# A two-layer hybrid decoder step: output gate stored as its silu, ten stream steps, the last taps and a score product moved

## The chip, the core and the metric

The kernel runs on one core of a Trainium2 chip. The metric is the device time of one execution in microseconds (us), the median of several. A core has a matrix engine (TensorE, PE in the profile; PEld is its weight load), three engines for element-wise work (VectorE or DVE, ScalarE or ACT, GpSimd or POOL) and SyncE (SP), which only issues transfers (DMA) here; ACT issues some too. Each engine carries out its own row of instructions in order, and waits where one needs a result of another engine or of a transfer.

## What is computed

Two layers over 1,104 tokens: 1,040 of a prompt and 64 of eight running sequences. In each layer the normalised input is projected to 8,260 columns, which feed three branches. Cut to what the change touches:

```
u = rmsnorm(h, norm_g) @ w_in + b_in           # af, aq, v(ai), az, ga, gg, bz, q, k, v, indexer, cz, gate
# branch A, HGRN2, four heads of 128 channels
q, k = silu(aq), (1 - lb) * sigmoid(-af);  o = gated linear recurrence(q, k, v, log f)
out_a = (norm(o) * silu(az)) @ w_pa            # az: the output gate
# branch B, Conformer convolution
y = silu(layernorm(conv31(ga * sigmoid(gg)) + conv_b))
out_b = ((y @ conv_pw) * silu(bz)) @ w_pb      # "pointwise products"
# branch C, sparse attention
s = sum over 4 heads of relu(qi_h . ki) * wi_h # indexer: scores; the 256 best keys are kept
out_c = (attention over the kept keys * silu(cz)) @ w_pc
h = h + (gate_a*out_a + gate_b*out_b + gate_c*out_c) @ w_out
```

## The kernel before

Channels lie on the 128 partitions, tokens along the free dimension, in three groups of 384, 384 and 336 (`NTS`). fp32 products are made of three fp32r ones (high by high, low by high, high by low). That is the dense **stream** (`stream`, L346): for each chunk of 128 channels and each group 24 matmuls into one of two PSUM buffers (`mm`), eight steps of three (L396). ACT evicts the buffer with the bias into an SBUF buffer (`sp`, L206 from L401) and, behind the third group, issues the store of the chunk to HBM itself (L411: `afD`, `aqD`, `vD`, `azD`, `czD`, ...). The weights of a chunk are split by ACT (`wh`, L271) and POOL (`wl`, L272). For a `cz` chunk the stream also makes the silu: a second ACT pass over the PSUM buffer gives the sigmoid into another `sp` buffer, and POOL multiplies.

PE's row is written out in program order. All other stages run on PE between pieces of the stream: `fill(key)` issues as many stream steps as the table `FILL` has for that key. Long DVE work is metered in the same way: `SIDE` has a budget in ns for each place, in which `taps(key)` issues taps of the convolution and `masks(key)` steps of the mask building. The order on DVE is that of the program in most stages, and that on ACT in a few; a scheduler sets the rest, so a changed table moves rows on these engines too.

The stages of a layer, in order, as far as they matter:

- **Indexer** (`indexer`, L759). For six blocks of queries and four heads PE makes scores (`lg`), ACT the relu (`rl`), and DVE multiplies by the head's weight and adds up (`SC`; the first head by L840, the others by L842). Then four copies and four subtractions make `qt8` (L853 to L858). For the eight running sequences the cached keys are gathered, scored and summed over heads by a product of PE (`gather`, L860 to L871) in two halves: DVE adds `lg` and `ac` to `SC` (L870, L871) after each. L908 is PE's next product and reuses the PSUM buffer `lg`. All the while DVE runs the **taps** of the convolution: 31 for each of four channel chunks, L1594 over the prompt and L1595 over the sequences, into `cy`. The last tap of a chunk is followed by its store `yD[c]` on SP (L1597).
- **Layer norm of the convolution** (`conv_norm`, L1602). For each token group SP loads `ny` from `yD`, two channel chunks a time (L1608), POOL adds the four chunks (L1611, L1612: `nsq`), PE sums over partitions (L1615), DVE and ACT go on, and SP stores the result (L1634).
- **Four heads** of the recurrence (`hgrn_head`, L1349). SP loads `hG`, `hQ`, `hT_` and `az`; ACT makes three sigmoids; POOL `sg = Q * sigmoid(Q)` (L1371); ACT and POOL `az * sigmoid(az)` (`sz`, L1376 to L1378); DVE products (L1400 to L1402), which ACT casts (`hl`, L1407).
- **Pointwise products** (`conv_out`, L1662). Three groups by four chunks of 12 matmuls on `BH` and `BL` (L289); DVE multiplies each result by silu(bz) (`bzt`, L1693), SP stores it; mask steps stand between (L1031 to L1040).
- **Attention** (`attention`, L1044). q goes through the rotary embedding (`rope_q`, L727: loads, DVE, stores on SP), k and v come back from HBM (`kr` and `vr`, L1056 and L1057, on ACT's queue), PE transposes `kr` (L1063), and the first scores are L1107.

## Time and profile before

| | |
|---|---|
| Median of 3 executions | 2865.78 us (2864.01 to 2873.34) |
| The profiled execution | 2876.56 us; its span in the trace 2874.7 us |
| Mean granted TensorE clock | 0.985 of full |
| PE busy | 2741.0 us, 95% of the span |
| DVE, ACT, POOL busy | 70%, 47%, 44% |
| PE waiting for ACT to evict a stream buffer | 33.0 us in 20 places, the longest 5.5 |

All rows come from the profiled execution, and times in them count from the start of its span. A row of a timeline has the start, the length, the engine, the line, the operation, the tiles written and read, shapes, and in brackets the idle time of that engine just before and what ended it. A row with the engine SPq or ACTq is the issue of a transfer. The first layer ends at about half of the span; the second repeats its stages.

### The profile page before, as it was taken

How to read it: one execution, taken by the hardware profiler on the slowest of the kernel's cores; microseconds unless marked ns; L12 is line 12 of the kernel's file. 1: busy time of each engine (PE TensorE's matmuls, PEld its weight loads, DVE VectorE, ACT ScalarE, POOL GpSimd, SP SyncE). 2: the span in 40 equal slices, each digit the busy share in tenths (PEclk: the TensorE clock that was granted, in tenths of full speed). 3: DMA queues.
4: the chain of work that ended last, by engine and by line, in shares of the span. 5: the costliest groups of instructions: out<-in, count | busy, mean ns of one | idle time of the engine just before them, and what ended most of it. 6: DMA issues, size and time to landing. Idle time of an engine off the chain costs nothing. (4 is left out here: it accounts for less than half of the span.)

```text
span 2874.7 us, 45280 instructions
## 1 busy us (share of the span) xinstructions
PE 2741.0 (95%) x17094; PEld 2607.7 (91%) x17094; DVE 2022.6 (70%) x3518; ACT 1357.9 (47%) x2913; POOL 1252.4 (44%) x1012
## 2 busy tenths in 40 slices
PE   7999989999998999999999999999999989999898
PEld 7999878999998998879999997899999989988798
DVE  5789966878986667545258699688888866774543
ACT  4324546773333556544342345577533245665432
POOL 3544344434424115756464352444444331168453
PEclk9999999999999999999999999999999999999999
DMA  4423233332344224665553232413331442257554
GB/s 149 158 83 113 91 123 121 120 120 98 107 155 150 76 68 151 211 199 175 161 166 108 81 102 99 166 68 117 130 131 62 160 152 76 84 157 234 180 155 151
DMA packets 192570, 374.16 MB, mean 130 GB/s; under 512 B 30656, under 2 KB 129696, under 8 KB 192288
## 3 DMA queue, kind: packets, MB, share of 16 engines
q1 hardware_dynamic: 161856, 270.11, 29.9%
q10 hardware_dynamic: 24608, 80.19, 7.1%
q0 software_dynamic: 5888, 20.97, 2.3%
q8 instruction: 134, 2.20, 0.3%
q14 instruction: 84, 0.69, 0.1%
HBM read 251.07 MB, written 122.40 MB: 130 GB/s over the span
## 5 line engine op out<-in xcount | busy, mean ns | idle before, releaser
L396 PE MATMUL mm<-xh,wh 128*128 128x384 f32 (+2 forms) x2656 | 889.5, 337 | 36.5 <-ACT sp L206 33.0
L396 PE MATMUL mm<-xl,wh 128*128 128x384 f32 (+2 forms) x2656 | 884.9, 336 | 0.0
L272 POOL TENSOR_TENSOR wl<-wr,wh 128x512 fp32r<-128x512 f32 x332 | 483.9, 1474 | 748.4 <-ACT wh L271 468.2
L396 PEld LDWEIGHTS mm<-xh,wh 128*128 128x128 f32 x2656 | 506.3, 191 | 50.8 <-ACT sp L206 40.2
L396 PE MATMUL mm<-xh,wl 128*128 128x384 f32 (+2 forms) x2656 | 525.3, 333 | 0.0
L396 PEld LDWEIGHTS mm<-xl,wh 128*128 128x128 f32 x2656 | 506.3, 191 | 6.9 <-issue 1.4
L396 PEld LDWEIGHTS mm<-xh,wl 128*128 128x128 f32 x2656 | 455.3, 190 | 6.2 <-issue 1.4
L206 ACT ACTIVATE sp<-mm,vec 128x384 f32<-128x384 f32 (+1 forms) x356 | 198.4, 564 | 386.4 <-PE mm L396 371.4
L1009 DVE TENSOR_SCALAR_CACHE_REDUCE jk<-SC,F 128x1024 uint8<-128x1024 f32 (+6 forms) x320 | 334.2, 1044 | 7.8
L1594 DVE SCALAR_TENSOR_TENSOR cy<-up,vec,cy 128x1040 f32<-128x1040 f32 x240 | 336.9, 1404 | 0.5
L271 ACT CAST wh<-wr 128x512 fp32r<-128x512 f32 x352 | 204.3, 617 | 116.3 <-PE mm L396 42.1
L206 ACT ACTIVATE P<-P,nm 128x896 f32<-128x896 f32 (+7 forms) x128 | 99.5, 778 | 72.8 <-DVE nm L1114 70.9
L1130 DVE TENSOR_TENSOR pl<-tp,ph 128x512 fp32r<-128x512 f32 x144 | 97.6, 686 | 36.1 <-ACT ph L1129 35.3
L1595 DVE SCALAR_TENSOR_TENSOR cy<-us,vec,cy 128x64 f32<-128x64 f32 x240 | 118.4, 493 | 0.0
L206 ACT ACTIVATE ja<-SC,hB,hz 80x1104 int8<-80x1104 int16 (+1 forms) x120 | 111.4, 929 | 0.2 <-issue 0.2
L1129 ACT CAST ph<-tp 128x512 fp32r<-128x512 f32 x144 | 83.2, 584 | 54.6 <-PE tp L1126 50.1
L1114 DVE CUSTOM_DVE_ANT_0 P<-sc,MB 128x512 f32<-128x512 f32 (+1 forms) x96 | 63.9, 667 | 55.2 <-PE sc L1108 54.2
L1118 DVE TENSOR_SCALAR P<-P,nm 128x896 f32<-128x896 f32 (+7 forms) x128 | 88.9, 695 | 4.2
L1126 PE MATMUL tp<-ident,P 128*128 128x128 f32 x576 | 87.5, 274 | 1.5 <-DVE P L1118 1.5
L206 ACT ACTIVATE rl<-lg 128x1024 f32<-128x1024 f32 (+6 forms) x54 | 42.6, 789 | 88.9 <-DVE SC L842 35.6
L1107 PE MATMUL sc<-KD,Q 128*128 128x512 f32 (+2 forms) x208 | 71.0, 344 | 11.8 <-DVE Q L1088 7.9
L289 PE MATMUL tp<-xh,wh 128*128 128x384 f32 (+2 forms) x240 | 80.3, 337 | 0.4 <-DVE z L1780 0.4
(472 smaller groups left out, 6072.5 us busy)
## 6 DMA issues: line engine op xcount, KB each, us to landing
wr<-in_wp SPq DMA_DIRECT2D x180, 512.0 KB
eg<-gateD SPq DMA_DIRECT2D x80, 184.0 KB
gateD<-sp ACTq DMA_DIRECT2D x24, 552.0 KB
gateD<-sp ACTq DMA_DIRECT2D x24, 544.0 KB
cr<-in_wc SPq DMA_DIRECT2D x16, 290.0 KB
gt<-gateD SPq DMA_DIRECT2D x24, 192.0 KB
za<-zaD SPq DMA_DIRECT2D x24, 192.0 KB
ggD<-sp ACTq DMA_DIRECT2D x8, 552.0 KB
```

Of the source, the lines that this page charges most:

```text
L206: S.activation(out, in_, fn, **kw)
L271: S.copy(wh[:, k:k + 4], wr[:, k:k + 4])
L272: (eng or G).tensor_tensor(wl[:, k:k + 4], wr[:, k:k + 4], f(wh[:, k:k + 4]), op=OP.subtract)
L289: T.matmul(ps[:, 0:nn], wk, x, start=(n == 0), stop=(n == 3 * K - 1))
L396: T.matmul(ps, w, x, start=(j == 0), stop=(j == 23))
L1009: V.tensor_scalar(jk[0:rows, 0:n], s, F.bitcast(F32)[0:rows, j:j + 1], None, op0=OP.is_ge, op1=OP.add, accum_out=cnt[0:rows, j:j + 1])
L1118: V.tensor_scalar(p[:, 0:n], p[:, 0:n], nm[:, 3:4], None, op0=OP.mult)
L1126: T.transpose(ps[:, 128 * c:128 * c + 128], P[c][:, 128 * kt:128 * kt + 128], ident)
L1129: S.copy(ph, ps)
L1130: V.tensor_tensor(pl, ps, f(ph), op=OP.subtract)
L1594: V.scalar_tensor_tensor(yp, up[:, j:j + 1040], w, yp, op0=OP.mult, op1=OP.add)
L1595: V.scalar_tensor_tensor(ys, us[:, :, j:j + 8], w, ys, op0=OP.mult, op1=OP.add)
```

## The change

Five edits in one. The two tables `FILL` and `SIDE` move ten stream steps from ahead of the pointwise products (`c0`) to ahead of the first attention scores (`aq`), give the fourth call pair of the taps in the sequences' scores (`ts`) a smaller budget, and give the mask steps other budgets. `az` chunks are made into their silu in the stream, as `cz` ones are, and the heads no longer do it. The first head's score product goes to GpSimd. The copies of `qt8` come ahead of their subtractions. In head 0 `sg = Q * sigmoid(Q)` goes to DVE.

```diff
--- before.py
+++ after.py
@@ -46,13 +46,13 @@
 
 FILL = {"n0": 10, "n1": 3, "n2": 0, "s0": 7, "s1": 0, "s2": 3, "ic": 35, "ik": (0, 3, 7), "iq": 7, "is": (6, 4, 7, 6, 7, 7),
         "iw": 13, "ib": 6, "ir": 3, "ig": 4, "na": (16, 6, 4, 8, 9, 4, 2, 12, 6), "h0": (63, 30, 39, 31), "hv": 6, "hd": 7,
-        "hl": (5, 6, 5, 5, 9, 6, 16), "hk": 2, "hs": (0, 1, 0, 1, 0, 1, 0, 4), "ho": 2, "ht": 10, "c0": 59,
-        "c1": (13, 22, 52), "aq": 16, "av": (2, 2, 2, 2, 2, 1, 3, 2), "a0": 6, "as": (3, 1, 1, 1, 2, 1, 0, 1),
+        "hl": (5, 6, 5, 5, 9, 6, 16), "hk": 2, "hs": (0, 1, 0, 1, 0, 1, 0, 4), "ho": 2, "ht": 10, "c0": 49,
+        "c1": (13, 22, 52), "aq": 26, "av": (2, 2, 2, 2, 2, 1, 3, 2), "a0": 6, "as": (3, 1, 1, 1, 2, 1, 0, 1),
         "mp": (3, 3, 3), "tl": 3, "tk": 4, "ts": (1, 2, 0, 2, 2), "tt": (0, 0, 1, 4, 6), "tp": (2, 2, 2, 1, 4, 3), "to": 1}
 SIDE = {"t0": (5000, 10000, 10000, 10000, 9300, 10000), "tr": (2400, 2400, 2400, 2400, 2400, 2400, 2400, 600, 0),
-        "tk": 4200, "ti": (1400, 2400, 2400, 2400, 2400, 2400), "ts": 5800,
+        "tk": 4200, "ti": (1400, 2400, 2400, 2400, 2400, 2400), "ts": (5800, 5800, 5800, 3000),
         "na": (3000, 3000, 0, 0, 0, 0, 0, 0, 0), "hd": 2000, "hl": (3000, 500, 1800, 1800, 3000, 3300, 7000),
-        "hs": 1000, "hk": 4000, "ho": 500, "ht": 2000, "he": 5500, "c0": 12000, "cc": 1200, "c1": 6000}
+        "hs": 1000, "hk": 4000, "ho": 500, "ht": 2000, "he": 5500, "c0": 14000, "cc": 1500, "c1": (2500, 4500, 6000)}
 KSEL = 4
 KEEP = 24
 EDGE = {mybir.EngineType.DVE, mybir.EngineType.Activation}
@@ -400,7 +400,7 @@
                     act_(bufs[i][:, sl], ps, fn, bias=pv[:, bcol + c:bcol + c + 1])
                     if behind[0]:
                         behind[0]()
-                    if nm in ("cz",):
+                    if nm in ("cz", "az"):
 
                         if g == 0:
                             sg = spt()
@@ -837,7 +837,7 @@
                     act_(rl[:, 0:n], ps[:, 0:n], AF.Relu)
                     taps("ti", 7 - i)
                     if h == 0:
-                        V.tensor_scalar(dst, rl[:, 0:n], wsc[:, i, 0:1], None, op0=OP.mult)
+                        G.tensor_scalar(dst, rl[:, 0:n], wsc[:, i, 0:1], None, op0=OP.mult)
                     else:
                         V.scalar_tensor_tensor(dst, rl[:, 0:n], wsc[:, i, h:h + 1], dst, op0=OP.mult, op1=OP.add)
                 dg = SC[:, SCOFF[i] + n - 128:SCOFF[i] + n]
@@ -855,6 +855,8 @@
             for h in range(4):
                 j, e = divmod(h, 2)
                 S.copy(qt8[0:64, h, :], (lo8 if e == 0 else hi8)[:, j, 0:16])
+            for h in range(4):
+                j, e = divmod(h, 2)
                 V.tensor_tensor(qt8[64:128, h, :], (lo8 if e == 0 else hi8)[:, j, 0:16], f(qt8[0:64, h, :]), op=OP.subtract)
             CH = ((0, 512), (512, 1024), (1024, NT))
 
@@ -879,11 +881,11 @@
                     ki = xt.tile([128, 1024], F32, name="kib", tag="kib", bufs=1)
                     for e in range(2):
                         kraw[e](ki[64 * e:64 * e + 64])
-                    taps("ts")
+                    taps("ts", 2 * g + b // 2)
                     if 4 * g + b < 6:
                         rows = [kidx_rows(l, 4 * g + b + 2 + e, xt) for e in range(2)]
                     fill("ib")
-                    taps("ts")
+                    taps("ts", 2 * g + b // 2)
                     fill("ib")
                     for n in range(2):
                         for e in range(2):
@@ -1368,14 +1370,11 @@
         act_(K, Gt, AF.Sigmoid, scale=-1.0)
         act_(Gt, Gt, AF.Sigmoid)
         act_(sg, Q, AF.Sigmoid)
-        G.tensor_tensor(sg, Q, sg, op=OP.mult)
+        (G if h else V).tensor_tensor(sg, Q, sg, op=OP.mult)
         if lbs[l] is not None:
             lb, ilb = lbs[l]
             V.tensor_scalar(K, K, ilb[:, h:h + 1], None, op0=OP.mult)
             V.tensor_scalar(Gt, Gt, ilb[:, h:h + 1], lb[:, h:h + 1], op0=OP.mult, op1=OP.add)
-        sz = h1.tile([128, NT], F32, name="sz", tag="St")
-        act_(sz, az, AF.Sigmoid)
-        G.tensor_tensor(az, az, sz, op=OP.mult)
         tof = {1: Gt, 2: TT[:, 0:552], 4: TT[:, 552:828], 8: TT[:, 828:966], 16: TT[:, 966:1031],
                32: TT[:, 1031:1063], 64: TT[:, 1063:1079], 128: TT[:, 1079:1087]}
 
@@ -1695,7 +1694,7 @@
                     masks("cc")
                 if g < 2:
                     nxt = rest()
-                masks("c1")
+                masks("c1", g)
                 fill("c1", g)
```

What the rows become. DVE's row at the end of the indexer, before: the last of the convolution's taps (L1594 and L1595 are one), then the sums of the first and of the second gather, then the search for the thresholds.

```order
L1594 SCALAR_TENSOR_TENSOR cy<-up,vec,cy 128x1040
L1595 SCALAR_TENSOR_TENSOR cy<-us,vec,cy 128x64
L870 TENSOR_TENSOR SC_1907<-SC_1907,lg 80x1024
L871 TENSOR_TENSOR SC_1907<-SC_1907,ac 80x80
L870 TENSOR_TENSOR SC_1907<-SC_1907,lg 80x1024
L871 TENSOR_TENSOR SC_1907<-SC_1907,ac 80x80
L1002 MEMSET cnt 128x3
```

And now, where lines behind L858 have numbers two higher and lines behind L1378 one lower:

```order
L872 TENSOR_TENSOR SC_1907<-SC_1907,lg 80x1024
L873 TENSOR_TENSOR SC_1907<-SC_1907,ac 80x80
L872 TENSOR_TENSOR SC_1907<-SC_1907,lg 80x1024
L873 TENSOR_TENSOR SC_1907<-SC_1907,ac 80x80
L1593 SCALAR_TENSOR_TENSOR cy<-up,vec,cy 128x1040
L1594 SCALAR_TENSOR_TENSOR cy<-us,vec,cy 128x64
...
L1004 MEMSET cnt 128x3
```

The last four taps (the first is shown, the dots stand for three more) are behind both sums. SP's row follows them; there before, from the store of the last chunk on:

```order
L1597 DMA yD<-cy 128x1104
L1608 DMA ny<-yD 128x2x384 x4
L1608 DMA ny<-yD 128x2x336 x2
L269 DMA wr<-in_wp 128x1024 x2
L1634 DMA yD<-ny 128x384 x4
```

And now, from the loads of the first two chunks on:

```order
L1607 DMA ny<-yD 128x2x384 x2
L1607 DMA ny<-yD 128x2x336
L269 DMA wr<-in_wp 128x1024
L1596 DMA yD<-cy 128x1104
L1607 DMA ny<-yD 128x2x384 x2
L1607 DMA ny<-yD 128x2x336
L269 DMA wr<-in_wp 128x1024
L1633 DMA yD<-ny 128x384 x4
```

The loads of chunks 0 and 1 are ahead of the last store, those of chunks 2 and 3 behind it. The third place is ACT's row at head 0 of the first layer; the `sp` rows of 384 and 336 are evictions of the stream. Before:

```order
L206 ACTIVATE sp<-mm,vec 128x384 x2
L206 ACTIVATE hK<-hG 128x1104
L271 CAST wh<-wr 128x512
L206 ACTIVATE hG<-hG 128x1104
L206 ACTIVATE sg<-hQ 128x1104
L206 ACTIVATE sp<-mm,vec 128x336
L271 CAST wh<-wr 128x512
L411 DMA azD<-sp 128x1104
L206 ACTIVATE sp<-mm,vec 128x384
L206 ACTIVATE sz<-az 128x1104
L1407 CAST hl<-sg 128x1104
L1407 CAST hl<-pr 128x552
```

Now:

```order
L206 ACTIVATE sp<-mm,vec 128x384 x3
L206 ACTIVATE hK<-hG 128x1104
L206 ACTIVATE sp<-mm,vec 128x384
L206 ACTIVATE hG<-hG 128x1104
L206 ACTIVATE sg<-hQ 128x1104
L206 ACTIVATE sp<-mm,vec 128x336 x2
L271 CAST wh<-wr 128x512
L411 DMA azD<-sp 128x1104
L271 CAST wh<-wr 128x512
L1406 CAST hl<-pr 128x552
L206 ACTIVATE sp<-mm,vec 128x384
L1406 CAST hl<-sg 128x1104
```

Three passes over PSUM (an eviction, its sigmoid and the next eviction) are ahead of `hK` instead of two, one stands between `hK` and `hG`, `sz` is gone, and the next chunk's first eviction is ahead of the cast of `sg`.

## Rows read from the trace of the kernel before

**Rows 1.** Waits of PE over the span: total us, times, longest.

```profile
PE lg L908 <- DVE SC L870: 5.0, 2, 2.5
...
PE lg L1442 <- POOL hK L1470: 2.6, 1, 2.6
```

**Rows 2.** Indexer, layer 1: L840 alone, then timeline of PE (start, length).

```profile
L840 DVE TENSOR_SCALAR SC<-rl,wsc x12: 405/574/740, 223.0 to 1725.3; 128x1024 f32<-128x1024 f32 x2, 128x896 f32<-128x896 f32 x2, 128x768 f32<-128x768 f32 x2, 128x640 f32<-128x640 f32 x2
...
313.86 1.56 PE L396 MATMUL mm<-xh,wl 128*128 128x384 f32 x8
...
316.65 0.42 PE L396 MATMUL mm<-xh,wh 128*128 128x336 f32 x1 [1.23 <-ACT sp L206]
```

**Rows 3.** Timeline of PE, 366 to 386 us, layer 1: end of the indexer.

```profile
369.31 0.45 PE L908 MATMUL lg<-KIH,qt 128*64 128x512 f32 x1 [2.50 <-DVE SC L870]
...
384.48 0.91 PE L1615 MATMUL tp<-nsq,ones 128*128 128x384 f32 x2 [0.63 <-POOL nsq L1612]
```

**Rows 4.** Timeline of DVE, same stretch.

```profile
366.64 1.29 DVE L1594 SCALAR_TENSOR_TENSOR cy<-up,vec,cy 128x1040 f32<-128x1040 f32 x1
...
368.05 1.21 DVE L870 TENSOR_TENSOR SC<-SC,lg 80x1024 f32<-80x1024 f32 x1
...
375.65 1.22 DVE L870 TENSOR_TENSOR SC<-SC,lg 80x1024 f32<-80x1024 f32 x1 [6.25 <-PE lg L865]
```

**Rows 5.** Timeline of SP and of POOL, same stretch.

```profile
368.15 0.33 SPq L1597 DMA_DIRECT2D yD<-cy  x1
375.79 2.94 SPq L1608 DMA_DIRECT2D ny<-yD  x6
...
380.37 1.85 POOL L1611 TENSOR_TENSOR nsq<-ny 128x768 f32<-128x768 f32 x1 [3.91 <-DMA ny<-yD]
...
383.43 1.00 POOL L1612 TENSOR_TENSOR nsq<-nsq 128x384 f32<-128x384 f32 x1
```

**Rows 6.** Timeline of POOL and of DVE, 254 to 258 us: two engines at once.

```profile
255.28 2.03 POOL L1576 TENSOR_TENSOR up<-up,cy 128x1040 f32<-128x1040 f32 x1 [0.94 <-DMA cy<-ggD]
...
255.87 2.53 DVE L1594 SCALAR_TENSOR_TENSOR cy<-up,vec,cy 128x1040 f32<-128x1040 f32 x1
```

**Rows 7.** Windows: length, then PE, PEld, DVE, ACT, POOL busy, PEclk, DMA share, GB/s.

```profile
370.00:373.40 3.40, 3.40 (x13) 3.11 (x11) 0.00 (x0) 1.14 (x2) 0.00 (x0) 0.50 0.10 40
458.80:465.60 6.80, 4.24 (x13) 4.24 (x14) 5.82 (x11) 5.85 (x18) 4.68 (x4) 0.50 0.01 6
1786.00:1792.00 6.00, 3.51 (x18) 2.58 (x17) 5.84 (x10) 0.58 (x1) 0.00 (x0) 1.00 0.15 63
```

**Rows 8.** Timelines of PE, ACT and DVE in head 0, layer 1.

```profile
446.72 0.45 PE L396 MATMUL mm<-xh,wh 128*128 128x384 f32 x1 [1.62 <-ACT sp L206]
...
461.36 0.69 PE L396 MATMUL mm<-xh,wh 128*128 128x384 f32 x1 [5.47 <-ACT sp L206]
...
442.57 1.13 ACT L206 ACTIVATE hK<-hG 128x1104 f32<-128x1104 f32 x1 [4.77 <-DMA hQ<-aqD]
...
455.57 1.11 ACT L1407 CAST hl<-sg 128x1104 fp32r<-128x1104 f32 x1 [6.49 <-DVE sg L1402]
...
460.75 0.56 ACT L206 ACTIVATE sp<-mm,vec 128x384 f32<-128x384 f32 x1
...
448.92 2.39 DVE L1400 TENSOR_TENSOR hQ<-sg,hG 128x1104 f32<-128x1104 f32 x1 [15.08 <-POOL sg L1371]
```

**Rows 9.** Timelines of PE and DVE around the pointwise products, layer 1.

```profile
863.80 0.45 PE L289 MATMUL tp<-BH,ph 128*128 128x384 f32 x1 [2.61 <-DVE bzt L1693]
...
842.36 0.56 DVE L1693 TENSOR_TENSOR bzt<-tp,bzt 128x384 f32<-128x384 f32 x1 [2.28 <-PE tp L289]
```

**Rows 10.** Timelines of PE and ACT at the start of attention, layer 1.

```profile
915.96 1.06 PE L1063 MATMUL tp<-ident,kr 128*128 128x128 f32 x8 [1.25 <-DMA kr<-kvD]
...
929.60 0.66 PE L1107 MATMUL sc<-KD,Q 128*128 128x512 f32 x1 [3.92 <-DVE Q L1088]
...
910.14 0.38 ACTq L1056 DMA_DIRECT2D kr<-kvD  x1
```
## The prediction

> **What bounds the kernel now.** I read the busy times first: PE is busy for 95% of the span (the table above), and the change takes no matmul away. So it can give back only what PE loses in waits and at half clock, and the list of PE's waits comes next. It has many kinds, most of a few us in all. Those in reach of the change are few: the wait of L908 for a sum on DVE, 5.0 us over both layers [rows 1], L1615 behind the layer norm's sums on POOL [rows 3], two waits of the stream in head 0 [rows 8], one among the pointwise products [rows 9], and two at the start of attention [rows 10]. The timeline of each then tells what was late. The windows show the price of a stall beyond its length: behind the 2.50 us of L908 the granted clock is 0.50 for 3.4 us, its lower level of 1.2 GHz, so 1.7 us of matmul time goes; behind the long wait of head 0 it is 0.50 for 6.8 us with PE busy for 4.24 us, so 2.1 us [rows 7]. The same L908 wait in the second layer leaves it at 1.00 [rows 7]. All other waits named here return in the second layer within 0.6 us, so terms are given per layer.
>
> **Edits that cost or give next to nothing.** *Score product.* Six products a layer, 0.74 us at most and 0.57 in the median, go from DVE to POOL [rows 2]; about 3.4 us of DVE a layer. DVE is not late again until the sum at 368.05, and there the moved taps decide, so 0. No row has this product on POOL. Its bounds: as long as on DVE, or the 2.53 us that one DVE tap takes beside a POOL sum of 2.03 [rows 6]; I take the nearer to the lower, since a tap is mostly alone. The dear end is a rival below. *The az silu* puts 24 sigmoids on ACT and 24 products on POOL a layer into the stream and takes four sigmoids and four products out of the heads. ACT is busy for 47% of the span (the table above), and the sigmoid stands behind the eviction that frees the PSUM buffer; 0, and as for loss, it is one eviction's length that the next one may be late by.
>
> *Copies of qt8.* Three copies no longer wait for a subtraction between them; PE's wait of 1.23 us behind them [rows 2] goes: **-1.2**.
>
> **Taps behind the sums.** Four taps leave DVE's row ahead of the sum that L908 waits for. One tap is 1.41 us from 366.64 to 368.05 [rows 4], four are 5.6 us, more than the 2.50 us [rows 3]: **-2.5**, and in the first layer **-1.7** for the clock.
>
> What is late next is the last tap itself. Its result is stored to HBM (368.15), read back (issued at 375.79, when the second gather has freed the memory), added up on POOL (380.37 for 1.85 us, then 1.00) and multiplied by L1615 [rows 3, 5]. Before, the store had over 7 us. Now the second sum ends about 4.2 us earlier than its 376.9 [rows 4], at 372.7; four taps lead to 378.3; the load of channels 2 and 3 can't start before the store has landed. A load takes 4.6 us from issue to POOL [rows 5]; the store has no row of its own in this place. For both together I bound 4.6 us (the load only) to 9.2 us (the store as long as the load) and take 6.4. With POOL's 2.85 us, L1615 starts at 387.6. PE would be there at 384.48 - 0.63 - 4.2 = 379.65 [rows 3]. The stall is 8.0 us in place of 0.63, +7.4, and as two of three stalls of this size or less drop the clock [rows 7], 1.7 more: **+9.1**. The cheap end is +5.6 (4.6 us, no clock). The dear end has each tap at 2.65 us (beside POOL, [rows 6]), 9.2 us of transfers and 1.3 us of POOL's other work: 396.6, with the clock +18.
>
> Taps run dearer beside POOL: 2.53 us against 1.29 [rows 4, 6]. The Trainium skill, SBUF — State Buffer, in "SBUF: two separate sides", has it that DVE and GpSimd share a pair of ports by an exclusive lock, which a DVE instruction with two SBUF inputs and a GpSimd instruction that reads SBUF hold for their whole length; the trace agrees, the tap above being longer by about what was left of the POOL sum. By it the four taps, now in a stretch with two weight splits on POOL, lose those splits' 2.6 us and no more, and the forecast would be 5 us later in all.
>
> **Head 0.** PE waits 5.47 us at 461.36 for an eviction (460.75) that stands behind a cast of sg in ACT's queue; that cast waited 6.49 us for DVE, whose first product waited for POOL's sg [rows 8]. With sg's product on DVE and no sz and az work, the stream's eviction stands ahead of that cast: -5.47, -2.1 of clock, and the 1.62 at 446.72 goes as well [rows 8]. But ACT's new order puts hK ahead of the fourth pass over the stream's PSUM buffers, and hK waits for its loads, 4.77 us of ACT idle before 442.57 [rows 8]. With two PSUM buffers about 1.5 us of it is covered: 3.3 us, and 1.7 for the clock. Net **-4.2**; the ends are -9.2 (no new stall) and -1 (the whole 4.77, and 3.4 of clock).
>
> **Heads 1 to 3.** POOL is freed of one product of 128x1104 a head; L1442 waited 2.6 us once for POOL's hK [rows 1]. Over two layers that is **-1.3** a layer; between 0 and -2.6.
>
> **Ten steps.** They are 30 matmuls at 0.174 us (eight in 1.56 us with the last one's length of 0.34 taken off, [rows 2]): 5.2 us. The products come earlier by that, but DVE's first one at 842.36 had 2.28 us of idle time only [rows 9] and now stands behind two more mask operations. I let PE wait 3 us in the first group; the wait of 2.61 in the second [rows 9] goes, as the masks that made it have moved ahead. The products then end about 2 us earlier. The rope, its store and the kr transfer hang on their end, so L1063 (which waited 1.25) and L1107 (3.92) [rows 10] are reached by PE as before relative to the products, with the ten steps in between as cover, but kr's issue (910.14) still waits for the chain. I take those 2 us as the gain: **-2**. The ends are -5.2 (both waits gone) and +5.2 (the products end no earlier, and nothing covers).
>
> **Sum.** Per layer -1.2 - 2.5 + 9.1 - 4.2 - 1.3 - 2 = -2.1; twice is -4.2; with the first layer's clock, -5.9 us. The profiled execution took 2876.56 us, so 2870.7 in its terms; that one was 0.4% above the median of the runs, 2865.78, and I carry the difference to the median: **2860 us**.
>
> **Rivals.** *The layer norm decides (slower).* The chain of tap, store, load and POOL at its dear end: +18 in place of +9.1 a layer, 8.9 more in each of two: -5.9 + 17.8 = +12, 2878. For it: no row shows the store's landing in this place, and a tap does double beside POOL [rows 6]. Against: the store is issued 0.1 us behind its tap [rows 4, 5], and in SP's new order only the first half's loads and one weight load stand right ahead of it. It makes the kernel slower by over 0.3% from about 395 us for L1615's start.
> *No new stall in head 0 (faster).* Three passes over the stream's buffers now stand ahead of hK, and PE may still be at work in the free buffer when hK's loads land. Then -5 more a layer: -5.9 - 10 = -16, 2850. Against it: those loads follow the layer norm's stores on SP, and the layer norm is later against PE.
> *The ten steps lose their place.* The products end no earlier, and attention starts as late as before: +5.2 in place of -2 a layer, 7.2 more in each: +8.5, 2874. For it: the first products wait for DVE, which has 2.28 us to spare and not 5.2.
> *The product on GpSimd is waited for.* It takes its place in POOL's row behind a mask select and ahead of the weight splits, so it holds those until ACT's relu is there, and DVE's second head waits for it. One stall of 3 us and 1.7 of clock a layer is 9.4 in all: +3.5, 2869. The Trainium skill, GPSIMD Engine Reference, section 3.1, puts GpSimd at about half of DVE's rate in element-wise work, which would make it 1.5 us at most; no run here shows it.
>
> **How the numbers follow.** The forecast has 0.42 and, by the cheap and dear ends of its small terms, 2851 to 2868; 0.3% of 2866 is 8.6 us, about what a measurement of this kernel can tell from no change, so 0.18 of it is faster and 0.24 the same. No new stall in head 0: 0.20, faster. The ten steps: 0.18, right on the bound, half of it slower. The layer norm: 0.12, slower. GpSimd: 0.08, of which 0.03 slower. Together 0.38 faster, 0.38 the same, 0.24 slower. The range runs from 2845, below the faster rival, to 2877, just short of the slower one.
>
> **What would show it.** L908 without a wait, and L1615 with one of 6 to 10 us and DVE's last tap some 9 us ahead of it, in both layers; the 5.47 us of head 0 gone, with a shorter one about 15 us ahead of its place; L1107 waiting less than 3.92 us. I am wrong if L1615 waits under 5 or over 15 us, if head 0 keeps its stall, or if PE waits for rl, wl or the split products in the score stage, where it did not before.

## The result

Before: 2866.25 us, median of 4 (2864.01 to 2873.34). After: **2915.13 us**, median of 4 (2912.55 to 2917.0). The ratio is 1.0154, 95% interval 1.0136 to 1.0171: slower by 1.5%, which is 44 us of 2866; the two medians lie 48.9 us apart. The profiled execution of the change took 2917.0 us, its span is 2914.9 us and its mean granted clock 0.976, against 0.985.

The busy times of the page, before and after, and the longest items in the new list of PE's waits (total us, times, longest):

```profile
PE 2741.0 (95%) x17094; PEld 2607.7 (91%) x17094; DVE 2022.6 (70%) x3518; ACT 1357.9 (47%) x2913; POOL 1252.4 (44%) x1012
PE 2749.6 (94%) x17094; PEld 2619.0 (90%) x17094; DVE 2017.7 (69%) x3508; ACT 1364.0 (47%) x2929; POOL 1282.6 (44%) x1038
```

```profile
PE mm L396 <- ACT sp L206: 48.0, 17, 8.6
PE tp L1614 <- POOL nsq L1611: 26.8, 2, 13.5
...
PE lg L805 <- ACT rl L206: 8.7, 2, 4.3
...
PE sc L1109 <- DVE Q L1090: 4.3, 2, 2.2
```

The wait of L908 [rows 1, 3] is gone. In its place L1614 (L1615 before) waits 13.4 us in each layer where it waited 0.63 [rows 3]; L805, which did not wait for relu, waits 4.3 us; and evictions cost 48.0 us in fewer places than the 33.0 of before. The half-clock windows around two of PE's stalls (13.4 us up to 395.38 and 8.2 us up to 911.00), in the columns of [rows 7]:

```profile
384.20:401.20 17.00, 5.83 (x16) 5.22 (x17) 7.13 (x12) 1.70 (x4) 8.52 (x7) 0.50 0.43 156
906.40:916.60 10.20, 5.60 (x20) 5.60 (x21) 3.65 (x3) 2.24 (x5) 1.97 (x2) 0.50 0.38 139
```

17.0 and 10.2 us at 1.2 GHz, the lower level, where the longest window of [rows 7] was 6.8. PE was busy for 5.83 and 5.60 us of them, so half of that, 2.9 and 2.8 us, is what the clock took beyond the stalls.

Where the time went is seen best from the starts of five products in PE's timelines, here as stage lengths in us (layer 1 / layer 2), worked out as differences of those starts. *Scores*: first L805 to L908. *Norm*: L908 to L1615. *Heads*: L1615 to the first pointwise product. *Attention start*: from there to the first L1107.

| kernel | scores | norm | heads | attention start |
|---|---|---|---|---|
| before | 150.9 / 150.4 | 15.2 / 13.8 | 455.5 / 454.8 | 89.6 / 88.4 |
| after | 151.8 / 152.0 | 26.3 / 26.4 | 447.1 / 448.7 | 107.4 / 107.1 |
| taps alone | 148.4 / 148.6 | 23.8 / 23.8 | 457.7 / 454.6 | 88.1 / 89.6 |
| taps, 20 steps ahead of the norm | 148.5 / 148.6 | 23.9 / 24.0 | 451.0 / 450.0 | 88.5 / 91.1 |
| silu of az alone | 156.9 / 156.8 | 14.9 / 14.9 | 456.3 / 455.3 | 87.8 / 90.9 |
| ten steps alone | 151.3 / 151.2 | 14.8 / 13.4 | 448.1 / 452.2 | 107.3 / 109.2 |
| ten steps, own scratch | 151.3 / 151.3 | 15.0 / 15.2 | 450.4 / 449.0 | 100.7 / 100.0 |
| ten steps, ACT's silu for cz | 151.3 / 150.5 | 15.0 / 15.2 | 448.7 / 451.6 | 97.1 / 96.3 |
| copies and sg alone | 150.6 / 149.8 | 14.9 / 13.5 | 456.2 / 451.9 | 88.9 / 90.1 |
| copies, sg, ACT's silu | 148.9 / 148.9 | 13.4 / 15.2 | 452.9 / 454.8 | 87.5 / 85.7 |

Ten steps are 5.2 us that leave "heads" for "attention start". In the changed kernel the norm is 11.1 and 12.6 us longer, the start of attention 17.8 and 18.7, the scores 0.9 and 1.6, and the heads 8.4 and 6.1 shorter: 48 us in all. The span grew by 40 only: the stretches outside these stages were 8 us longer in the profiled execution of before, which was itself 10 us above its median.

**The layer norm.** DVE, SP, POOL and PE in the changed kernel, first layer, which answer to [rows 3 to 5]:

```profile
375.09 1.29 DVE L1593 SCALAR_TENSOR_TENSOR cy<-up,vec,cy 128x1040 f32<-128x1040 f32 x1
...
381.11 2.34 DVE L1593 SCALAR_TENSOR_TENSOR cy<-up,vec,cy 128x1040 f32<-128x1040 f32 x1
383.37 0.91 DVE L1594 SCALAR_TENSOR_TENSOR cy<-us,vec,cy 128x64 f32<-128x64 f32 x1
...
384.31 0.33 SPq L1596 DMA_DIRECT2D yD<-cy  x1
389.00 1.40 SPq L1607 DMA_DIRECT2D ny<-yD  x3
...
376.33 1.12 POOL L408 TENSOR_TENSOR sp<-sp 128x384 f32<-128x384 f32 x1 [1.81 <-ACT sp L206]
378.99 3.36 POOL L272 TENSOR_TENSOR wl<-wr,wh 128x512 fp32r<-128x512 f32 x2 [1.53 <-ACT wh L271]
...
392.45 1.80 POOL L1610 TENSOR_TENSOR nsq<-ny 128x768 f32<-128x768 f32 x1 [8.25 <-DMA ny<-yD]
...
395.38 1.65 PE L1614 MATMUL tp<-nsq,ones 128*128 128x384 f32 x2 [13.37 <-POOL nsq L1611]
```

The four taps take 9.2 us (375.09 to 384.28), not 5.6: POOL's az product (376.33) and weight splits (378.99) run beside them. The store is issued 0.03 us after the last tap, the load that waits for it 4.7 us later, and POOL starts 3.45 us after that. From last tap to PE it is 11.1 us, and PE had nothing else in its row.

**The scores.** POOL, ACT and PE at one place of the score stage:

```profile
248.42 2.40 POOL L840 TENSOR_SCALAR SC<-rl,wsc 128x768 f32<-128x768 f32 x1 [2.11 <-ACT rl L206]
250.79 4.44 POOL L272 TENSOR_TENSOR wl<-wr,wh 128x512 fp32r<-128x512 f32 x2
255.19 0.89 POOL L408 TENSOR_TENSOR sp<-sp 128x336 f32<-128x336 f32 x1
...
256.11 0.33 ACTq L411 DMA_DIRECT2D azD<-sp  x1
256.48 0.37 ACT L797 CAST qs<-tp 64x256 fp32r<-64x256 f32 x1 [6.26 <-POOL SC L844]
...
258.11 0.80 PE L805 MATMUL lg<-KIH,qs 128*128 128x512 f32 x1 [4.33 <-ACT rl L206]
```

ACT issues the store of an az chunk (256.11) in its row, so it stands until POOL has made the last product of the chunk (255.19), which stands behind a weight split (250.79) and the score product (248.42, 2.40 us). The casts and the relu behind the store are 6.3 us late, and PE waits 4.33 us.

**The start of attention.** ACT and PE:

```profile
901.81 0.33 ACTq L411 DMA_DIRECT2D czD<-sp  x1
902.24 0.58 ACT L206 ACTIVATE sp<-mm,vec 128x384 f32<-128x384 f32 x1 [6.86 <-POOL sp L408]
910.36 1.52 ACT L206 ACTIVATE sp<-mm,vec 128x384 f32<-128x384 f32 x3 [7.54 <-DMA czD<-sp]
...
911.00 0.65 PE L396 MATMUL mm<-xh,wh 128*128 128x336 f32 x1 [8.24 <-ACT sp L206]
```

The pass over PSUM at 902.24 is the bias pass of a cz chunk's first group; the one at 910.36 is its sigmoid. It writes the silu's scratch, and that scratch is the other of the two `sp` buffers, the one whose store was issued at 901.81. The store has landed 8.5 us later, and until then two PSUM buffers are full and PE stands for 8.24 us. POOL's row shows why that store was issued so late, behind a product that stood behind a weight split:

```profile
894.60 5.33 POOL L272 TENSOR_TENSOR wl<-wr,wh 128x512 fp32r<-128x512 f32 x2 [8.49 <-PE mm L396]
899.88 1.90 POOL L408 TENSOR_TENSOR sp<-sp 128x336 f32<-128x336 f32 x1
```

In the kernel before, ACT's same pass stood as well, but PE lost 1.88 us only:

```profile
883.32 0.33 ACTq L411 DMA_DIRECT2D czD<-sp  x1
...
900.91 0.33 ACTq L411 DMA_DIRECT2D czD<-sp  x1
901.63 0.58 ACT L206 ACTIVATE sp<-mm,vec 128x384 f32<-128x384 f32 x1 [3.28 <-PE mm L396]
906.98 1.52 ACT L206 ACTIVATE sp<-mm,vec 128x384 f32<-128x384 f32 x3 [4.77 <-DMA czD<-sp]
...
907.61 0.42 PE L396 MATMUL mm<-xh,wh 128*128 128x336 f32 x1 [1.88 <-ACT sp L206]
```

PE in the changed kernel, further on:

```profile
929.09 0.42 PE L396 MATMUL mm<-xh,wh 128*128 128x336 f32 x1 [3.19 <-ACT sp L206]
...
931.63 1.91 PE L1065 MATMUL tp<-ident,kr 128*128 128x128 f32 x8
```

Both stalls of the changed kernel, 8.24 and 3.19 us, stand ahead of the transposes of `kr`, in the 52 steps of `c1`'s third group, whose number the change leaves as it was. The ten steps themselves stand in `aq`, behind the transposes. What they do to this stretch is to set the stream back by ten steps, so that other chunk ends fall between the last product and the transposes: one before (its store is the one at 900.91), two after (901.81 and 921.10). The 6.4 us that the first stall has grown by divide like this. Before, ACT was ahead: it waited 3.28 us for PE, and PE had 4.8 us of work left when the store was issued. After, ACT had stood 6.86 us for POOL's product, and PE had 0.95 us left; that makes 3.9 us. The other 2.5 us are the store's: from its issue to the sigmoid it is 8.55 us, for 6.07.

From the start of the last product to the transposes it was 30.0 and 28.8 us in the two layers and is 41.3 and 41.6; of these 11.3 us in the first layer 8.3 are waits and 2.8 the clock. From the transposes to the first scores it is 4.5 us more, the ten steps (5.2 us) with L1107 (now L1109) waiting 2.2 us for 3.92; the products take 2.0 us more.

### The profile page after: what moved, and what is told of

It is laid out like the page before. It is cut to its first block, busy times and chain, and to the rows that moved or that the text cites. A ratio compares the mean times of both kernels' runs of the same rounds, so it can differ in the third digit from the quotient of the medians.

```text
span 2914.9 us, 45326 instructions
## 1 busy us (share of the span) xinstructions
PE 2749.6 (94%) x17094; PEld 2619.0 (90%) x17094; DVE 2017.7 (69%) x3508; ACT 1364.0 (47%) x2929; POOL 1282.6 (44%) x1038
## 5 line engine op out<-in xcount | busy, mean ns | idle before, releaser
L272 POOL TENSOR_TENSOR wl<-wr,wh 128x512 fp32r<-128x512 f32 x332 | 492.2, 1500 | 750.6 <-ACT wh L271 419.5
L206 ACT ACTIVATE sp<-mm,vec 128x384 f32<-128x384 f32 (+1 forms) x380 | 210.3, 565 | 430.6 <-PE mm L396 372.4
L1594 DVE SCALAR_TENSOR_TENSOR cy<-us,vec,cy 128x64 f32<-128x64 f32 x240 | 127.2, 530 | 0.0
L408 POOL TENSOR_TENSOR sp<-sp 128x384 f32<-128x384 f32 (+2 forms) x48 | 53.7, 1126 | 87.0 <-issue 47.2
L1109 PE MATMUL sc<-KD,Q 128*128 128x512 f32 (+2 forms) x208 | 71.2, 345 | 8.2 <-DVE Q L1090 4.3
```

Source lines behind the costliest of these rows:

```text
L206: S.activation(out, in_, fn, **kw)
L272: (eng or G).tensor_tensor(wl[:, k:k + 4], wr[:, k:k + 4], f(wh[:, k:k + 4]), op=OP.subtract)
L1109: T.matmul(ps, Q[:, c, :], KD[k][:, c0:c1], start=True, stop=False)
L1594: V.scalar_tensor_tensor(ys, us[:, :, j:j + 8], w, ys, op0=OP.mult, op1=OP.add)
```

## The experiments

Each was timed against the kernel before on the same chip. Diffs are against the kernel before; lines that are the change's own are only named.

**1. Taps alone** (the change's `ts` lines). 

> The kernel before with only the smaller budget for the taps between the sequences' scores, so that the last taps stand behind the sums. Theory 1 (the chain last tap, store, load, sum on POOL is itself too long): L908 no longer waits, but the first product of the layer norm waits 9 to 12 us in each layer at half clock, 2878 to 2892 us. Theory 2 (the chain is long only because POOL's new az products slow the taps and delay POOL): a wait of 5 to 7 us, 2868 to 2875 us.

Measured: 2886.9 us, ratio 1.0067 (1.0051 to 1.0084). L908 waits no more and the scores are 2.2 us shorter in the mean of both layers, but the norm is longer by 9.3:

```profile
381.65 0.33 SPq L1597 DMA_DIRECT2D yD<-cy  x1
385.32 1.40 SPq L1608 DMA_DIRECT2D ny<-yD  x3
...
388.63 1.80 POOL L1611 TENSOR_TENSOR nsq<-ny 128x768 f32<-128x768 f32 x1 [8.30 <-issue]
...
391.56 1.65 PE L1615 MATMUL tp<-nsq,ones 128*128 128x384 f32 x2 [10.82 <-POOL nsq L1612]
```

Theory 1: the chain alone is 9.9 us from last tap to PE. The stall of the changed kernel is 2.5 us longer. There the four taps take 9.2 us for 7.8 here, with az products beside them (1.4), and the load is issued 4.7 us behind the store for 3.7 here (1.0). That this is POOL's new work holds for the taps; for the transfers no run shows it.

**2. Taps, with cover** (the `ts` lines and):

```diff
-        "iw": 13, ... "na": (16, 6, 4, 8, 9, 4, 2, 12, 6), "h0": (63, 30, 39, 31)
+        "iw": 13, ... "na": (36, 6, 4, 8, 9, 4, 2, 12, 6), "h0": (43, 30, 39, 31)
```

> The four taps behind the sums, as in the run of it alone, with twenty stream steps moved from head 0 to ahead of the layer norm's second products. Theory 1 (the wait for the last tap's store and load is pure latency): 10.4 us of other matmuls do not help the first product if they stand behind it, so its wait of 10.8 us stays and the time is 2876 to 2892 us; the steps only help if PE reaches them first, then 2862 to 2872 us. Theory 2 (head 0 needs those steps): waits in head 0 grow by 3 us or more a layer, above 2890 us.

Measured: 2875.2 us, 1.0016 (1.0004 to 1.0028). PE reaches the twenty steps first, and L1615 waits 0.96 us:

```profile
388.29 0.91 PE L1615 MATMUL tp<-nsq,ones 128*128 128x384 f32 x2 [0.96 <-POOL nsq L1612]
```

So the wait is latency that matmuls in the right place cover. But the time lies just below the range for steps that do not help, and 3 us above the one for steps that do. The heads pay a part of it back: 451.0 and 450.0 us, where 10.4 us less than in run 1 would be 447.3 and 444.2.

**3. Silu of az alone** (the `az` lines). 

> The kernel before with only the silu of az made in the stream. Theory 1 (the az store on ACT's queue waits for POOL's product and holds what stands behind it, relu and evictions): a new wait in the score stage or the layer norm of some us, eaten up by head 0's 5.5 us that go: 2862 to 2872 us. Theory 2 (it needs the score product on POOL as well for a stall): only head 0's gain is left, 2845 to 2858 us.

Measured: 2885.3 us, 1.0056 (1.0039 to 1.0074), beyond what either theory gave: the scores are 6 us longer in each layer, and head 0 gains next to nothing, its wait is 4.57 us for 5.47. Of the 6 us in the scores PE's new or longer waits give 4.0:

```profile
256.68 0.50 PE L805 MATMUL lg<-KIH,qs 128*128 128x512 f32 x1 [1.64 <-ACT rl L206]
...
310.55 0.45 PE L396 MATMUL mm<-xh,wh 128*128 128x384 f32 x1 [2.74 <-ACT sp L206]
...
375.25 0.45 PE L908 MATMUL lg<-KIH,qt 128*64 128x512 f32 x1 [3.34 <-DVE SC L870]
```

The kernel before has 1.23 us of waiting for an eviction in this stage and 2.50 at L908, and none for the relu. In head 0 the cast of sg no longer holds ACT; the next instruction does, `ja`, which waits 3.98 us for DVE's threshold search, and the eviction stands behind it.

**4. The same, az stored from GpSimd's queue:**

```diff
-    S.dma_start(fD[nm][c, :, lo:NT], bufs[i][:, lo:NT])
+    (G if nm == "az" else S).dma_start(fD[nm][c, :, lo:NT], bufs[i][:, lo:NT])
```

> The silu of az in the stream, as in the run of it alone, but the az chunks stored by GpSimd's queue instead of ACT's. Theory 1 (the store on ACT waits for GpSimd's product and holds the relu and the evictions behind it): the waits for relu (1.6 us) and eviction (2.7 us) in the score stage go, 2862 to 2874 us. Theory 2 (GpSimd's and ACT's added work itself is late): they stay, 2880 to 2890 us.

Measured: 2883.4 us, 1.0037 (1.0024 to 1.005). The wait for relu falls from 1.64 us to two of 0.56, so it was the store's place in ACT's row; but the wait for an eviction stays (2.76 for 2.74 us), and the scores take 156.7 us still. What keeps them long, the second pass over PSUM, POOL's products or the stores that now stand in GpSimd's row, this run does not separate: with these stores a product of the norm waits 3.3 us, and the heads are 2.6 us longer than in run 3. That is near theory 2, with theory 1's wait shown for the relu alone.

**5. Silu of az and score product on GpSimd** (the `az` and `G.tensor_scalar` lines). 

> The silu of az in the stream and the first head's score product on GpSimd together, nothing else of the change. Theory 1 (the product lies in GpSimd's row ahead of the weight split and the az product, whose store holds ACT's row): PE waits 4 us or more for relu in the score stage of each layer, which neither edit alone made, and the time is 2884 to 2895 us. Theory 2 (no interplay): a wait of 1 to 2 us, 2878 to 2886 us.

Measured: 2885.7 us, 1.0048 (1.0031 to 1.0066). The 4.33 us are there, which neither edit made alone:

```profile
258.20 0.50 PE L805 MATMUL lg<-KIH,qs 128*128 128x512 f32 x1 [4.33 <-ACT rl L206]
```

But the time is that of run 3: the scores take 156.7 us, as the wait of 2.74 us for an eviction is gone in exchange. The interplay explains the wait, not a loss of its own.

**6. Score product alone.** 

> The kernel before with only the first head's score product on GpSimd. Theory 1 (harmless by itself, POOL has room): 2862 to 2870 us, no new wait of PE in the score stage. Theory 2 (it delays the weight splits and, through relu, ACT): a wait of 2 to 4 us for relu or evictions in each layer, 2872 to 2880 us.

Measured: 2868.5 us, 0.9999 (0.9986 to 1.0012): theory 1's time, though PE does wait for the relu in the scores, 1.0 us once in each layer; the stage is no longer for it (150.2 and 150.3 us). The product itself is dear, 2.6 us in the median on POOL:

```profile
L840 POOL TENSOR_SCALAR SC<-rl,wsc x12: 2401/2591/3872, 218.9 to 1713.8; 128x1024 f32<-128x1024 f32 x2, 128x896 f32<-128x896 f32 x2, 128x768 f32<-128x768 f32 x2, 128x640 f32<-128x640 f32 x2
```

**7. Ten steps alone** (`c0`, `aq`, and the mask budgets). 

> The kernel before with only the ten steps moved from ahead of the pointwise products to the start of attention, and the mask budgets that go with them. Theory 1 (in the start of attention the stream runs no faster than its stores land, so ten more steps there are ten steps of waiting): PE's wait for an eviction grows from 1.9 to about 8 us in each layer, 2874 to 2886 us. Theory 2 (that wait came from POOL's other new work, and the steps are cover): 2856 to 2866 us.

Measured: 2896.7 us, 1.0101 (1.0084 to 1.0118), more than theory 1 gave. ACT's rows repeat the picture of the changed kernel without any of its other edits:

```profile
889.93 0.33 ACTq L411 DMA_DIRECT2D czD<-sp  x1
890.36 0.58 ACT L206 ACTIVATE sp<-mm,vec 128x384 f32<-128x384 f32 x1 [6.19 <-POOL sp L408]
898.81 1.52 ACT L206 ACTIVATE sp<-mm,vec 128x384 f32<-128x384 f32 x3 [7.87 <-DMA czD<-sp]
...
899.44 0.65 PE L396 MATMUL mm<-xh,wh 128*128 128x336 f32 x1 [7.90 <-ACT sp L206]
```

PE had 1.6 us of work left at the store's issue, and the buffer came free 8.9 us behind it. The second chunk end makes PE wait 3.6 and 4.1 us more in the two layers, and from the last product to the transposes of `kr` it is 41.7 and 42.1 us. So the place of the stall is shown by this run; of its two parts the later store is read from rows, and why the release takes longer is open (the loads of the rotary embedding are issued in the microseconds before, which no run took away). Nor does any run part the steps from the mask budgets that move with them.

**8. Ten steps, cz stored in three parts by GpSimd's queue:**

```diff
+    if nm == "cz":
+        G.dma_start(fD[nm][c, :, sl], bufs[i][:, sl])
-    if g == 2:
+    elif g == 2:
```

> The ten steps moved, as in the run of the steps alone, and each cz chunk stored in three parts by GpSimd's queue, one behind each product, instead of one store of the whole chunk on ACT's queue. Theory 1 (the silu's scratch is the buffer whose store has just been issued, and the stream stands until that store has landed): the first two parts have landed long before, so PE's wait of 8 us for an eviction falls to 4 us or less in each layer and the time to 2876 to 2888 us. Theory 2 (the wait belongs to the loads and stores of the rotary embedding that fill the queues there, whatever the store): 2893 to 2903 us.

Measured: 2892.5 us, 1.0081 (1.0061 to 1.0101); the waits are 6.6 and 6.8 us. Neither theory's number. The sigmoid now waits for the last third, and from its issue that alone took 7.4 us to release the buffer, where the whole chunk in run 7 took 8.9. The stores are also in another engine's row now, so the run leaves the question open.

**9. Ten steps, scratch of its own** (and two pools of attention with one buffer less; shortened, `scr[0]` is the pool `mbp` in this stage):

```diff
-    if g == 0:
-        sg = spt()
-    act_(sg[:, sl], ps, AF.Sigmoid, ...)
-    G.tensor_tensor(bufs[i][:, sl], bufs[i][:, sl], sg[:, sl], op=OP.mult)
+    if scr[0]:
+        sv = scr[0].tile([128, 384], F32, name="sv", tag="sv", bufs=1)[:, 0:nn]
+    ...
+    act_(sv, ps, AF.Sigmoid, ...)
+    G.tensor_tensor(bufs[i][:, sl], bufs[i][:, sl], sv, op=OP.mult)
```

> The ten steps moved, and the silu of cz gets a scratch tile of its own of 384 columns instead of the stream's second buffer; to make room, two pools of attention get one buffer less (8 to 7 for the exponentials, 6 to 5 for the tail's values). Theory 1 (the next chunk's first sigmoid waits for the store of the chunk before, because the scratch is that chunk's buffer): the waits of 7.9 and 8.5 us at the start of attention fall to 2 us or less, and from the pointwise products to the first scores a layer takes 95 us or less instead of 107 to 109. Theory 2 (the stores and loads of that stretch hold the stream in any case): 104 us or more. The smaller pools may cost some us in attention, so the whole time can be 2870 to 2890 us either way.

Measured: 2882.1 us, 1.0038 (1.0024 to 1.0052). The wait falls to 3.43 us in the first layer and is gone in the second, and the start of attention is 6.6 and 9.2 us shorter than in run 7 (34.3 and 33.9 us from the last product to the transposes): the shared buffer was that part. But 100 us lies between the two forecasts, for the next waits have come up; in the second layer L1070 waits 7.46 us, for which the trace names no cause. First layer:

```profile
908.29 0.42 PE L397 MATMUL mm<-xh,wh 128*128 128x336 f32 x1 [3.43 <-ACT sv L207]
914.60 1.94 PE L1070 MATMUL tp<-ident,kr 128*128 128x128 f32 x8 [4.19 <-DMA qD<-rD]
```

**10. Ten steps, ACT's silu for cz:**

```diff
-    act_(sg[:, sl], ps, AF.Sigmoid, ...)
-    G.tensor_tensor(bufs[i][:, sl], bufs[i][:, sl], sg[:, sl], op=OP.mult)
-    fn = AF.Sigmoid if ...
+    fn = AF.Silu if nm in SILU else AF.Sigmoid if ...      # SILU = ("cz",)
```

> The ten steps moved, and the silu of cz made by ScalarE's own silu function in one pass over PSUM, without sigmoid, scratch and GpSimd product. Theory 1 (scratch and store): the waits of 8 us go, the stretch from the pointwise products to the first scores takes 95 us or less, 2855 to 2872 us. Theory 2 (transfers hold the stream in any case): 104 us or more, 2885 to 2897 us.

Measured: 2871.8 us, 1.0007 (0.9997 to 1.0017), with 97.1 and 96.3 us for the start of attention: at the end of theory 1's range for the time and just beyond its 95 us. Without scratch and POOL product the kernel with the ten steps is level with the one before. Transposing `kr` waits in each layer, in the first for a transfer of the rotary embedding, in the second with no cause named:

```profile
911.55 1.48 PE L1061 MATMUL tp<-ident,kr 128*128 128x128 f32 x8 [3.11 <-DMA qD<-rD]
...
2331.29 1.27 PE L1061 MATMUL tp<-ident,kr 128*128 128x128 f32 x8 [4.57 <-issue]
```

The run changes the silu as well, and no run has this silu of cz without the steps, so what the steps cost by themselves is not shown. Run 14, with it and without the steps, reaches the transposes in 28.1 and 28.6 us, for 31.4 and 30.5 here.

**11. Copies and sg alone.** 

> The kernel before with only the four copies ahead of the four subtractions and head 0's product of Q on DVE instead of GpSimd. Theory 1 (head 0's wait of 5.5 us comes from GpSimd's product): it falls by 2 to 5 us in each layer, and the indexer's 1.2 us goes, 2852 to 2862 us. Theory 2 (the wait comes from ACT's row and only moves): 2863 to 2870 us.

Measured: 2860.6 us, 0.9966 (0.9951 to 0.9981): theory 1's time. Its mechanism is not borne out. Head 0's wait is 4.11 us in the first layer and split into 1.54 and 2.47 in the second, some 1.4 us a layer less where 2 to 5 were expected; the indexer's 1.23 us is not gone but stands further ahead, at 307.15 us, and is 1.64. The stages of the table are 2.7 us shorter together in the profiled execution. So where the 9.8 us come from stays open.

**12. The changed kernel without its `ts` lines.** 

> The changed kernel with the taps back ahead of the sums. Theory 1 (GpSimd's new az products slow the last taps, so the taps cost more here than alone): 24 us or more are gained, 2891 us or less. Theory 2 (same cost as alone): 16 to 22 us are gained, 2893 to 2899 us.

Measured: 2897.6 us, 1.0087 (1.007 to 1.0105), against 1.0154 with them: the taps cost 0.67% here as alone. Theory 2.

**13. Two taps behind the sums, ten steps of cover** (with the copies and sg; budget 4400 for 3000, `na` 26 and `h0` 53). 

> The small edits (copies ahead of subtractions, head 0's product of Q on DVE) with two taps instead of four behind the sums and ten stream steps moved from head 0 to ahead of the layer norm's second products. Theory 1 (the last tap's chain is latency that other matmuls cover, and two taps suffice for L908's 2.5 us): no wait at L908 and at most 3 us at the layer norm, 2852 to 2862 us. Theory 2 (head 0 misses the steps): 2863 us or more.

Measured: 2870.1 us, 0.9998 (0.9988 to 1.0008). The norm's wait is 2.23 us as expected, but what the scores and head 0 won goes in later waits of the heads: 7.22 us for an eviction in the second layer. Theory 2.

**14. Copies, sg, and ACT's silu for az and cz** (the diff of run 10 with both in `SILU`, and the heads' three `sz` lines removed); no ten steps, no moved taps, no product on GpSimd. 

> The small edits and the silu of az and cz made by ScalarE's silu function in the stream, the heads without sigmoid and product of az. Theory 1 (what az cost was the store behind GpSimd's product and the second pass): the score stage is as short as before, 151 us, and head 0's wait shorter, 2845 to 2860 us. Theory 2 (the table loads that silu needs, twelve more of 1.28 us, stand ahead of evictions): 2862 us or more.

Measured: **2856.4 us, 0.9949 (0.9932 to 0.9967)**: it beats both kernels, by theory 1's time. What the silu adds to run 11's 0.9966 is not clear of noise, as the two intervals overlap. The scores are 1.5 to 2 us shorter than before, and head 0's two waits [rows 8] are one of 3.29 us. The table loads of ACT are 52 in place of 38, at 1.28 us each; no wait of PE is put down to one.

## Why the prediction was wrong

The forecast was 2860 us with a range to 2877; it came out 38 us above the range. Edit by edit the ratios of the single runs are +0.67% (taps), +0.56% (az), +1.01% (steps), 0 (product) and -0.34% (copies and sg), 1.9% in sum against 1.54% measured together. In us the miss is about 50, the forecast having been a gain of 6. By the single runs 33 are the ten steps (29 slower, for 4 faster), 16 the az silu, 8 the taps and the norm and some 4 head 0 and its neighbours, 10 more than they make together.

- **The step that failed: the ten steps, put at -2 us a layer.** The term reasons with the end of the products, the chain to kr and the steps as cover, and takes the stretch between products and kr as it was. Alone the steps cost 29 us, 14.5 a layer (run 7), and that stretch went from 30.0 and 28.8 us to 41.7 and 42.1. There the stream, set back by ten steps, meets other chunk ends, and the sigmoid behind each needs the buffer whose store was just issued: PE stood 7.90 us in the first layer. A scratch buffer of its own (run 9) takes 15 us of the 29 away, 6.6 and 9.2 of them at this place; ACT's silu (run 10), with neither scratch nor POOL product, takes all of it, though what that silu wins by itself was not measured. The row was in the trace, ACT idle for 4.77 us behind a czD transfer and PE for 1.88, and the prediction's list of waits has neither. Of its two waits in reach L1107's did fall, from 3.92 to 2.2 us, as its sign asked, and it did not pay. The rival "the ten steps lose their place" had the place and the sign right, the cause wrong, and its +5.2 us a layer, 10.4 in all, is a third of the 29.
- **The az silu, put at 0.** Alone it cost 16 us. It is 24 sigmoids and products over both layers, not in each as the prediction has it: ACT has 16 instructions more, 24 less the eight that left the heads. I weighed the second pass over PSUM and not the store's place, in ACT's row behind a product on POOL. Run 4 shows that part for the relu's wait; the 6 us a layer in the scores are there in both runs, and which of passes, products and stores makes them was not separated. ACT's own silu, with one pass and no product, costs nothing there (run 14). The sign "PE waits for rl in the score stage" came true, 4.33 us in each layer.
- **The layer norm: mechanism right, size off.** Forecast: a stall of 8.0 us and L1615 9.1 us dearer with the clock. Measured: 13.4 us of stall, and a stage longer by 11.1 and 12.6 us where these terms make 5.7 and 7.4 (what is won at L908 lies in the stage before, and the clock behind the stall in the one after). The 5.4 us more of stall are the taps, 9.2 us for 5.6, and the transfers, 8.1 for 6.4. The clock took 2.9 us for 1.7. The rival "the layer norm decides" put its bound at about 395 us for L1614's start, and it came at 395.38: the taps alone are 0.67% slower (run 1). By the Trainium skill, SBUF — State Buffer, "SBUF: two separate sides", the taps would lose POOL's instructions that stand beside them; run 1 agrees, 2.2 us lost beside 2.6 us of weight splits. The az products of the change, 1.4 us more, were not in my count.
- **L908 and the copies.** In the change the 2.5 us and the 1.23 us are gone, and so is the first layer's clock window. L908 is right by run 1 too. For the copies run 11 does not bear it out: with them, and no tap moved, the 1.23 us come back as 1.64 in another place.
- **Head 0: too much.** The 9.8 us of copies and sg alone (run 11) are near the 10.8 that these terms make (twice 1.2 and 4.2), but by luck as far as the rows go: the waits there fell by 1.4 us a layer and not 4.2. In the change head 0 still waits 1.90 and 3.50 us in the first layer and 3.44 and 2.95 in the second, for [rows 8] 1.62 and 5.47: the second eviction has got past the cast of sg, as forecast, and stands behind `ja`, which waits 4.01 us for DVE.

```profile
467.86 1.22 ACT L206 ACTIVATE ja<-SC,hB 80x1104 int8<-80x1104 int16 x1 [4.01 <-DVE hB L964]
...
469.59 0.56 ACT L206 ACTIVATE sp<-mm,vec 128x384 f32<-128x384 f32 x1
```

- **Heads 1 to 3, put at -1.3 a layer: failed.** The wait for POOL's `hK`, 2.6 us once, is there twice:

```profile
PE lg L1441 <- POOL hK L1469: 3.7, 2, 2.4
```

- **The score product: 0, right** (run 6; run 5 against run 3 shows no time from it either, though it makes the relu's wait). But a product takes 2.4 us in the median there, near my dear bound and four times DVE's 0.57. The Trainium skill, GPSIMD Engine Reference, section 3.1, has GpSimd 1.96 times slower in an add of two tensors. This product reads one, and here the measurement decides; what of it DVE's instructions beside it add was not separated.

What stays open: why the silu of az keeps the 2.7 us eviction wait when its store leaves ACT's row; why a store's buffer is released later in the changed kernel than before; and where run 11's gain comes from. The parts add up to 0.36%, about 10 us, more than the whole, which is within what the five intervals allow together.

## What to carry to other kernels

Filler work is not free-standing. Moving steps of a stream from one place to a later one shifts every chunk boundary between the two, and so decides which stores and evictions fall where nothing else covers them. Before it is moved, ask for each boundary in such a bare stretch which buffer its next step needs, and what must land before that buffer is free: here a stall of 1.9 us became one of 8.2 in steps that the change had not touched. A store that an in-order engine issues makes all behind it wait for the engine that makes the data: here ACT stood 6.26 us and PE 4.33. And a result that goes through HBM, here with two sums on POOL behind it, had 9.9 us (run 1) and 11.1 us (the change) between its last instruction and its first reader on the matrix engine. As much other work has to stand in the matrix engine's row ahead of that reader.

## What the runs showed of the hardware

- From the issue of a store of a whole chunk to the sigmoid that waits for its buffer it was 6.1 us before, 8.5 in the change and 8.9 in run 7, and 7.4 us for a third of a chunk (run 8), all at one place, the start of attention.
- Around a stall of PE of 13.4 us the granted clock was 1.2 GHz for 17.0 us, around one of 8.2 us for 10.2 us.
- ScalarE has a silu function that did the work of a sigmoid pass, a buffer and a GpSimd product. In the kernel with it, ACT loaded its tables 52 times for 38, at 1.28 us each, and the time was 0.9949 of before's (run 14).
